# Input projection of a hybrid transformer layer: context after latents, small parameter work after the first norms, modulation pieces two at a time

## The chip, the cores and the metric

The kernel runs on one core of a Trainium2 chip. The metric is the time of one execution on the device in microseconds (us); less is better. The core has five engines that run side by side, each through its own queue in order: PE (TensorE, matrix products), DVE (VectorE), ACT (ScalarE), POOL (GpSimd) and SP (SyncE, which here only issues transfers). They meet through semaphores.

## The reference

One layer over 512 latent tokens (`x`) with a prefix of 256 context tokens (`ctx`), width 1024. The part that the change touches:

```python
m_lat = jax.nn.silu(c) @ w_mod[l] + b_mod[l]          # 6*1024 columns: shift, scale, gate, twice
m_ctx = jax.nn.silu(c_ctx) @ w_mod[l] + b_mod[l]
h_lat = modulate(rmsnorm(x, norm_mix_g[l]), sh1, sc1)     # t * (1 + scale) + shift
h_ctx = modulate(rmsnorm(ctx, norm_mix_g[l]), csh1, csc1)
p_lat = h_lat @ w_in                                   # columns: q 256, kv 128, kr 32, lru x 512, lru gate 512
p_ctx = h_ctx @ w_in
```

From `p_lat` and `p_ctx` come latent attention (queries of the latents only; keys and values of both) and a bidirectional recurrent block (`lru`), then the output projection, a router and 64 experts with 256 hidden columns each, eight of them per token, and a last norm. Nothing of this computation changes.

## The kernel before

Activations are held transposed: 128 channels on the partitions, eight channel tiles k, and 768 token columns, the 512 of the latents (0 to 511) and the 256 of the context behind them. Every product of the input projection is made from two-part numbers: weights and activations are split into a high and a low part (`split`: a cast, then a subtraction), and `mm3` (L357) makes three products, high·high, high·low and low·high, each in two instructions, one of 512 columns for the latents (L362) and one of 256 for the context (L364).

The first stage goes like this. `load_x` (L252) loads two token tiles into one of six "big" buffers. `norm1` (L293) squares each tile on ACT, makes the inverse root with twelve small DVE instructions (`rsqrt`, L150) and scales the tiles on DVE (L299). `trx` (L323) transposes a channel tile of all its token tiles on PE (L326) and copies it out of PSUM, ACT for even k, DVE for odd (L327). `mod1` (L307) makes the shift and scale columns of two channel tiles from two "big" weight tiles `wm1` (64 small products on PE, L311, then a transpose and two DVE instructions up to `mcolA`, L319). `hmake` (L385) applies them: ACT writes the high part `hH` (L388), POOL the full value `hfull` (L390), DVE their difference `hL` (L392). It does both token groups of a channel tile in one call. `kvproj` (L395) and `qproj` (L400) then add one channel tile into the PSUM tiles `pkv`, `pkr` and `pqq`, which fill all three wide PSUM buffers (`pw`, L228); there is one narrow buffer (`pn`, L231). `wtile` (L342) splits weights.

Afterwards the pool `pH`, with the six big buffers and the transposed activations, is closed (L422), and pools that take its memory are opened. In them lie the weights of the recurrent block's gates (`gv`, 16 loads issued by POOL, L474, split by POOL into `gH`, `gL`), the buffers of the modulation pieces and the temporaries. Then come four full projections of the `lru` columns (`proj`, L366, tiles `pp`, the first one `plx[0]` with weights `wl0`, the second with `wl1`), four of the gate columns for the latents alone (`lgp`, L629), convolutions, gates and scans.

Between them stand 16 modulation pieces (`mod_piece`, L444): each adds 1/8 of the products of 2048 further modulation columns, as four groups of 32 PSUM partitions (L454). In the trace a group is two matmul records. A piece loads the piece after next when it is done (L461), from 1 MB of weights in two transfers. Before the change 13 pieces stand one by one in the code and the last three in `mod_piece(16)` (L705).

SP's queue runs in the order in which the code is written (L109), which is the order of the loads: `x`, `wkv`, the first `wm1` pair, `ctx`, `wq`, three `wm1` pairs, `C2` and `C4` (two further parts of `w_in`). The queues of PE, ACT, DVE and POOL are ordered when the kernel is built, by a planner that takes the ready instruction of the highest priority by its own estimates of times; priority is the place in the code, moved by the offsets in `PRI` (L60). At run time nothing is reordered.

Of the kernel before, what the change touches and what calls it, by code (L numbers as in the profile page):

```python
# [8 lines left out]
F32 = mybir.dt.float32  # L9
# [3 lines left out]
AF = mybir.ActivationFunctionType  # L13
OP = mybir.AluOpType
# [86 lines left out]
def tile_kernel(tc, x, c, ctx, c_ctx, w_mod, b_mod, norm_mix_g, w_in, q_norm_g, w_q_up, kv_norm_g, w_kv_up,  # L101
# [17 lines left out]
    def pick(name, default):  # L119
        return {"A": ACT, "D": DVE, "P": POOL}[ENG.get(name, default)]  # L120
# [5 lines left out]
    def after(ins, other, reason):  # L126
        tc.add_manual_dep(ins, other.name, mybir.DependencyInfo(mybir.DependencyClass.Sync, mybir.DependencyReason.DATA),
                          reason=reason)

    def prio(name):  # L130
        def deco(f):
            def g(*args, **kw):
                off = PRI.get(name, 0)
                if not off:
                    return f(*args, **kw)
                with tc.high_priority(offset=off):
                    return f(*args, **kw)
            return g
        return deco
# [88 lines left out]
    def pw(name="pw"):  # L228
        return ps.tile([P, 1024], F32, tag="w", name=name, bufs=3)
# [31 lines left out]
    def load_win(c0, n):  # L261
        w = raw8("win")
        v = w.rearrange("p (k f) -> p k f", k=KT)[:, :, :n]
        SP.dma_start(v, w_in[0].rearrange("(k p) f -> p k f", p=P)[:, :, c0:c0 + n])
        return v

    wkv = load_win(C_KV, 160)
    wm1 = {}

    def load_wm1(c):  # L270
        for x_ in range(2):
            w = big("wm1").rearrange("p (k f) -> p k f", k=KT)
            SP.dma_start(w, wmv[:, :, x_ * D + c * 256:x_ * D + (c + 1) * 256])
            wm1[c, x_] = w

    load_wm1(0)
    load_x(ctx[0], 2)
    wq = load_win(0, 256)
    for c in range(1, 4):
        load_wm1(c)  # L280
    C2 = load_win(C_LX, 256)
    C4 = load_win(C_LG, 256)

# [37 lines left out]

    @prio("trx")
    def trx(k, t0, t1):  # L323
        pt = pw("pt")
        for t in range(t0, t1):
            PE.transpose(pt[:, (t - t0) * P:(t - t0 + 1) * P], xn[t][:, k * P:(k + 1) * P], ident)  # L326
        (DVE.tensor_copy if k % 2 else ACT.copy)(xnT[:, k, t0 * P:t1 * P], pt[:, 0:(t1 - t0) * P])  # L327

    for k in range(KT):
        trx(k, 0, NT)  # L330
    norm1(NT, NTA)
    pc = pn("pc")
    PE.transpose(pc[:, :P], prow, ident)
    DVE.tensor_copy(pcol[:, :ncol], pc[:, :ncol])
# [22 lines left out]
    def mm3(p, wt, k, first, last, lat=True, cx=True):  # L357
        hv, lv = wt
        for i, (w, m) in enumerate(((hv, hH), (hv, hL), (lv, hH))):
            st, sp = first and i == 0, last and i == 2  # L360
            if lat:
                PE.matmul(p[:, 0:S], w[:, k, :], m[:, k, 0:S], start=st, stop=sp)  # L362
            if cx:
                PE.matmul(p[:, S:ST], w[:, k, :], m[:, k, S:ST], start=st, stop=sp)  # L364
# [4 lines left out]
            mm3(p, wt, k, k == 0, k == KT - 1, cx=cx)  # L369
        return p  # L370

    for k in range(KT):
        trx(k, NT, NTA)
    wqt = []
    for m in range(2):
        z = pK.tile([P, 2, KT, P], F32R, tag=f"qw{m}", name="wqs", bufs=1)
# [4 lines left out]
    wl0 = z  # L381
    pkv, pkr, pqq = pw("pkv"), pw("pkr"), pw("pqq")

    @prio("hmake")
    def hmake(k):  # L385
        tt = hf("hfull")[:, 0:ST]
        for s, a, b in ((0, 0, S), (1, S, ST)):
            ACT.activation(hH[:, k, a:b], xnT[:, k, a:b], AF.Identity, scale=mcolA[:, k, s:s + 1],  # L388
                           bias=mcolS[:, k, s:s + 1])
            pick("hm", "P").tensor_scalar(tt[:, a:b], xnT[:, k, a:b], mcolA[:, k, s:s + 1], mcolS[:, k, s:s + 1],  # L390
                               op0=OP.mult, op1=OP.add)
        DVE.tensor_tensor(hL[:, k, :], tt, hH[:, k, :].bitcast(F32), op=OP.subtract)  # L392

    @prio("kvproj")
    def kvproj(k):  # L395
        mm3(pkv, kvt, k, k == 0, k == KT - 1)
        mm3(pkr, krt, k, k == 0, k == KT - 1)

    @prio("qproj")
    def qproj(k):  # L400
        for m in range(2):
            for i, (w, h_) in enumerate(((wqt[m][0], hH), (wqt[m][0], hL), (wqt[m][1], hH))):
                PE.matmul(pqq[:, m * S:(m + 1) * S], w[:, k, :], h_[:, k, 0:S],
                          start=(k == 0 and i == 0), stop=(k == KT - 1 and i == 2))
# [3 lines left out]
    for c in range(4):  # L408
        if c < 3:
            mod1(c + 1)  # L410
            hmake(2 * c + 2)
            hmake(2 * c + 3)
        kvproj(2 * c)
        if c < 3:
            qproj(2 * c)
        kvproj(2 * c + 1)
        if c < 3:
            qproj(2 * c + 1)
    qproj(6)
    qproj(7)  # L420
    load_brow(1)
    st_H.close()  # L422
    st_Z = ExitStack()
# [60 lines left out]

    @prio("small_params")
    def small_params():
        DVE.tensor_scalar(pcol[:, col["qg"]:col["qg"] + 2], pcol[:, col["qg"]:col["qg"] + 2], SCALE, None, op0=OP.mult)
        DVE.tensor_scalar(bh, pcol[:, col["ba"]:col["ba"] + 16], 0.5, None, op0=OP.mult)
        DVE.scalar_tensor_tensor(sm[0], lam, -1.0, lam, op0=OP.mult, op1=OP.max)
        ACT.activation(sm[1], sm[0], AF.Exp, scale=-1.0)  # L490
        DVE.tensor_scalar(sm[0], sm[1], 2.0, None, op0=OP.add)
        DVE.reciprocal(sm[2], sm[0])
        DVE.tensor_tensor(sm[0], sm[1], sm[2], op=OP.mult)
        DVE.tensor_tensor(sm[1], sm[0], sm[0], op=OP.mult)
        DVE.tensor_scalar(sm[2], sm[1], 1.0 / 17.0, None, op0=OP.mult)
        for nn in (15, 13, 11, 9, 7, 5, 3):
            DVE.scalar_tensor_tensor(sm[2], sm[2], 1.0 / nn, sm[1], op0=OP.add, op1=OP.mult)
        DVE.scalar_tensor_tensor(sm[2], sm[2], 1.0, sm[0], op0=OP.add, op1=OP.mult)
        DVE.tensor_scalar(sm[3], lam, -1.0, 0.0, op0=OP.mult, op1=OP.max)
        DVE.scalar_tensor_tensor(sm[3], sm[2], 2.0, sm[3], op0=OP.mult, op1=OP.add)  # L500
        DVE.tensor_scalar(spp, sm[3], 4.0, None, op0=OP.mult)
        DVE.tensor_scalar(spn, sm[3], -4.0, None, op0=OP.mult)
# [88 lines left out]
    plx = {}  # L591
    plx[0] = proj(wl0)
    wl1 = wtile(C2, P, "l1")
    mod_piece()
    pss = pn("pss")
    for t in range(NTA):
        PE.matmul(pss[:, t:t + 1], sqk[:, t * P:(t + 1) * P], ones[:, 0:1], start=True, stop=True)
# [8 lines left out]
    rsqrt(pL, nr, nv, 10, "rq")  # L606
    conv_b(0)
    plx[1] = proj(wl1)
    mod_piece()
    for i in range(LT):  # L610
        split(gH[:, i], gL[:, i], gvs[i][:, 0:4 * P], "gw")
    wg = wtile(C4, 0, "g0")
# [25 lines left out]
        ACT.activation(h_, h_, AF.Tanh)  # L638
        DVE.scalar_tensor_tensor(x_, h_, 1.0, x_, op0=OP.add, op1=OP.mult)

    mod_piece()
    lgp(0, wg)
    split(kvnH, kvnL, kvr, "kvn")
    for m in range(2):
# [2 lines left out]
    zs = gates_pe(0, 1)  # L647
    conv_b(1)
    gates_ew(0, 1, zs)
    mod_piece()  # L650
    plx[2] = proj(wl2)
    wg = wtile(C4, P, "g1")
    C5 = load_win(C_LG + 256, 256)
    mod_piece()
    zs = gates_pe(1, 0)
    gates_ew(1, 0, zs)
    conv_a(2, plx[2])
    mod_piece()
    lgp(1, wg)
    wl3 = wtile(C3, P, "l3")  # L660
    mod_piece()
    zs = gates_pe(1, 1)
    conv_b(2)
    gates_ew(1, 1, zs)
    mod_piece()
    plx[3] = proj(wl3)
    wg = wtile(C5, 0, "g2")
    wkvraw = raw8("wkvraw")[:, 0:1024]
# [2 lines left out]
    scan(0, 0)  # L671
    scan(0, 1)
    scan(1, 0)
    mod_piece()
    zs = gates_pe(2, 0)
    conv_a(3, plx[3])
    gates_ew(2, 0, zs)
    scan(1, 1)
    mod_piece()
    lgp(2, wg)  # L680
    wg = wtile(C5, P, "g3")
    wqraw = raw8("wqraw").rearrange("p (k h d) -> p k h d", k=2, h=H)
# [2 lines left out]
    for half in range(2):  # L685
        o, i = (wqraw[:, :, :, c0:c0 + 32].rearrange("p k h (a x j) -> p k h a x j", a=2, x=2)[:, :, :, :, x]
                for c0, x in ((DQK, half), (NOPE, 1 - half)))
        for k in range(2):
            POOL.tensor_copy(o[:, k], i[:, k])
    mod_piece()  # L690
    zs = gates_pe(2, 1)
    conv_b(3)
    gates_ew(2, 1, zs)
    mod_piece()
    zs = gates_pe(3, 0)
    gates_ew(3, 0, zs)
# [930 lines left out]
```

## Time and profile before

| | us |
|---|---|
| median of 3 runs | 1115.57 (1115.56 to 1118.78) |
| the profiled execution | 1114.81 |
| its span, first to last instruction | 1112.8 |
| PE busy | 996.2 (90%) |
| DVE, ACT, POOL busy | 484.3, 255.7, 223.4 |
| mean granted PE clock | 0.962 of full speed |

Times in rows count from the span's start. A row of a timeline gives start, duration, engine, line, operation, output and inputs, shapes, how many instructions were merged, and in brackets how long the engine had been idle before and what ended that. Matmuls overlap, so the pace of a stream is read from the starts, not from the durations.

### The profile page before, as it was taken

How to read it: one execution, taken by the hardware profiler on the slowest of the kernel's cores; microseconds unless marked ns; L12 is line 12 of the kernel's file. 1: busy time of each engine (PE TensorE's matmuls, PEld its weight loads, DVE VectorE, ACT ScalarE, POOL GpSimd, SP SyncE). 2: the span in 40 equal slices, each digit the busy share in tenths (PEclk: the TensorE clock that was granted, in tenths of full speed). 3: DMA queues.
4: the chain of work that ended last, by engine and by line, in shares of the span. 5: the costliest groups of instructions: out<-in, count | busy, mean ns of one | idle time of the engine just before them, and what ended most of it. 6: DMA issues, size and time to landing. Idle time of an engine off the chain costs nothing. (4 is left out here: it accounts for less than half of the span.)

```text
span 1112.8 us, 17435 instructions
## 1 busy us (share of the span) xinstructions
PE 996.2 (90%) x6813; PEld 515.6 (46%) x6813; DVE 484.3 (44%) x1064; ACT 255.7 (23%) x468; POOL 223.4 (20%) x219
## 2 busy tenths in 40 slices
PE   3899989799989998999999999999999999995482
PEld 2687654567779853443443344333333333331131
DVE  5527594988765865223222232222322223220065
ACT  3433545756661210011000110000100001000011
POOL 3382341346100001111111111111111111110001
PEclk9899999889999999999999999999999999997797
DMA  9834644200009543999999898989879999989694
GB/s 294 266 96 154 206 161 133 77 1 1 1 2 365 226 195 132 416 394 417 419 409 360 333 390 346 395 323 399 339 289 401 399 413 414 399 319 414 251 421 186
DMA packets 75404, 310.34 MB, mean 279 GB/s; under 512 B 12747, under 2 KB 31234, under 8 KB 48442
## 3 DMA queue, kind: packets, MB, share of 16 engines
q1 hardware_dynamic: 60412, 271.79, 63.2%
q0 software_dynamic: 13936, 34.26, 8.1%
q10 hardware_dynamic: 974, 3.17, 0.8%
q8 instruction: 54, 0.88, 0.3%
q14 instruction: 28, 0.23, 0.1%
HBM read 293.31 MB, written 30.29 MB: 291 GB/s over the span
## 5 line engine op out<-in xcount | busy, mean ns | idle before, releaser
L1382 PE MATMUL gu<-wgu,hT 128*32 128x512 f32 (+2 forms) x2160 | 333.0, 597 | 11.1 <-DMA wgu<-in_exp_w_up_dram 10.4
L1382 PEld LDWEIGHTS gu<-wgu,hT 128*32 128x32 f32 (+2 forms) x2160 | 105.4, 120 | 230.2 <-issue 225.9
L1403 PE MATMUL dn<-wd,aT 128*32 128x512 f32 (+2 forms) x1080 | 169.1, 596 | 16.6 <-ACT aT L124 15.4
L1385 DVE TENSOR_TENSOR act<-act,gu 128x256 f32<-128x256 f32 (+1 forms) x46 | 19.4, 421 | 297.8 <-ACT act L1384 297.8
L1384 ACT ACTIVATE act<-gu 128x256 f32<-128x256 f32 (+1 forms) x46 | 17.7, 385 | 511.7 <-PE gu L1382 511.7
L1332 POOL DMA_INDIRECT hg<-h2d,bix x46 | 47.6, 1034 | 425.9 <-issue 310.4
L1406 DVE SCALAR_TENSOR_TENSOR y<-dn,bw,g2b 128x1024 f32<-128x1024 f32 (+1 forms) x46 | 59.0, 1283 | 138.2 <-PE dn L1403 138.2
L1403 PEld LDWEIGHTS dn<-wd,aT 128*32 128x32 f32 (+2 forms) x1080 | 48.7, 119 | 100.8 <-issue 78.8
L1407 POOL DMA_INDIRECT yd<-y,biy x46 | 46.8, 1017 | 191.9 <-DVE y L1406 182.5
L1370 PEld LDWEIGHTS tr<-ident,hg 128*128 128x128 f32 (+1 forms) x368 | 39.9, 141 | 37.1 <-issue 34.1
L1370 PE MATMUL tr<-ident,hg 128*128 128x128 f32 (+1 forms) x368 | 49.7, 278 | 1.3 <-DVE tb L1084 1.3
L1548 PE MATMUL fs<-yl,ident 128*128 128x512 f32 x64 | 32.1, 654 | 20.3 <-DMA yl<-yd 18.1
L829 PE MATMUL pTr<-ident,P 128*128 128x128 f32 x192 | 30.7, 300 | 9.8 <-DVE P L820 7.7
L1306 DVE TENSOR_TENSOR sv<-iot,posR 128x256 bf16<-128x256 f32 (+3 forms) x93 | 37.1, 411 | 0.0
L812 DVE TENSOR_REDUCE nm<-pS 128x1 f32<-128x768 f32 x32 | 30.3, 951 | 11.2 <-PE pS L810 10.8
L124 ACT COPY PT<-pTr 128x384 f32<-128x384 f32 x64 | 28.0, 482 | 29.0 <-PE pTr L829 28.7
L124 ACT COPY hT<-tr 128x512 f32<-128x512 f32 (+1 forms) x46 | 26.9, 584 | 34.0 <-PE tr L1370 32.5
L840 PE MATMUL po<-PT,vsb 128*64 128x128 f32 x384 | 30.8, 299 | 1.7 <-ACT PT L124 1.7
L454 PE MATMUL pmx<-wm,csil 128*32 128x512 f32 x128 | 31.9, 606 | 0.0
L124 DVE COPY hT<-tr 128x512 f32<-128x512 f32 (+1 forms) x46 | 31.3, 680 | 0.0
L1548 PEld LDWEIGHTS fs<-yl,ident 128*128 128x128 f32 x64 | 12.7, 208 | 39.8 <-DMA yl<-yd 20.4
L829 PEld LDWEIGHTS pTr<-ident,P 128*128 128x128 f32 x192 | 24.1, 153 | 14.8 <-issue 7.7
(473 smaller groups left out, 1472.9 us busy)
## 6 DMA issues: line engine op xcount, KB each, us to landing
wgu<-in_exp_w_gate_dram SPq DMA_DIRECT2D x64, 1024.0 KB
wgu<-in_exp_w_up_dram SPq DMA_DIRECT2D x64, 1024.0 KB
wd<-in_exp_w_down_dram SPq DMA_DIRECT2D x64, 1024.0 KB
wm<-in_w_mod_dram SPq DMA_DIRECT2D x32, 512.0 KB
yl<-yd SPq DMA_DIRECT2D x16, 1024.0 KB
wm<-in_w_mod_dram SPq DMA_DIRECT2D x8, 1024.0 KB
win<-in_w_in_dram SPq DMA_DIRECT2D x5, 1024.0 KB
xz<-in_x_dram SPq DMA_DIRECT2D x4, 512.0 KB
```

The costliest lines, as they stand in the source:

```text
L124: (e.copy if e is ACT else e.tensor_copy)(dst, src)
L454: PE.matmul(pm[32 * g:32 * g + 32, :], csil[:, kk, :], wmp[n, g // 2][:, (g % 2) * 512:(g % 2 + 1) * 512], start=(kk == 0), stop=(kk == KT ...
L829: PE.transpose(p[:, j * P:(j + 1) * P], Pm[u][:, k * P:(k + 1) * P], ident)
L840: PE.matmul(po[i][64 * hh:64 * hh + 64, t * P:(t + 1) * P], vsb[:, k, 2 * i + hh, :], PTt[i, t, hh][:, k, :], start=(k == 0), stop=(k == N ...
L1306: DVE.tensor_tensor(sv[:, :, c:c + w], iot[:, u:u + w][:, None, :].to_broadcast([P, NT, w]), col_[:, :, None].to_broadcast([P, NT, w]), op ...
L1332: POOL.indirect_dma_start(out=b.hg[0:m], out_offset=None, in_=h2d, in_offset=bass.IndirectOffsetOnAxis(ap=b.ix[0:m, :1], axis=0), bounds_c ...
L1370: PE.transpose(p[:, i * m:(i + 1) * m], b.hg[0:m, (i0 + i) * P:(i0 + i + 1) * P], ident[0:m, 0:m])
L1382: PE.matmul(p[c:c + w, :], b.hT[:, k, c:c + w], wg[n][:, :, k, :], start=(k == 0), stop=(k == KT - 1))
L1403: PE.matmul(p[c:c + w, n0:n0 + 512], b.aT[:, k, c:c + w], wd_[n][:, k, n0:n0 + 512], start=(k == 0), stop=(k == 1))
L1406: DVE.scalar_tensor_tensor(y[0:m], p[0:m], b.w[0:m], g2b[0:m], op0=OP.mult, op1=OP.mult)
L1407: ins = POOL.indirect_dma_start(out=yd, out_offset=bass.IndirectOffsetOnAxis(ap=b.iy[0:m, :1], axis=0), in_=y[0:m], in_offset=None, bounds ...
L1548: PE.matmul(p[:, n0:n0 + 512], ident, yl[t, k][:, n0:n0 + 512], start=(k == 0), stop=(k == 3))
```

## The change

The load of `wkv` goes behind the first `wm1` pair and the load of `ctx` behind the last. The norm, the transposes, the modulation and the key/value products of the context are taken out of the latents' loop and follow it, channel tile by channel tile; the context's transposes use the narrow PSUM buffer. Four small DVE instructions that begin the parameter work of the recurrent block get a dependency on the second `hL` of the latents. The pieces that stood one by one now stand in six pairs, and the last four are left for `mod_piece(16)`.

```diff
-    wkv = load_win(C_KV, 160)
...
     load_wm1(0)
-    load_x(ctx[0], 2)
+    wkv = load_win(C_KV, 160)
     wq = load_win(0, 256)
     for c in range(1, 4):
         load_wm1(c)
+    load_x(ctx[0], 2)
     C2 = load_win(C_LX, 256)
...
-        pt = pw("pt")
+        pt = (pw if t0 == 0 else pn)("pt")
...
         trx(k, 0, NT)
-    norm1(NT, NTA)
...
-    for k in range(KT):
-        trx(k, NT, NTA)
...
+    hm = []
+
     @prio("hmake")
-    def hmake(k):
+    def hmake(k, s=0):
         tt = hf("hfull")[:, 0:ST]
-        for s, a, b in ((0, 0, S), (1, S, ST)):
...
+        a, b = ((0, S), (S, ST))[s]
...
+        hm.append(DVE.tensor_tensor(hL[:, k, a:b], tt[:, a:b], hH[:, k, a:b].bitcast(F32), op=OP.subtract).ins)
...
-    def kvproj(k):
-        mm3(pkv, kvt, k, k == 0, k == KT - 1)
-        mm3(pkr, krt, k, k == 0, k == KT - 1)
+    def kvproj(k, s=0):
+        mm3(pkv, kvt, k, k == 0, k == KT - 1, lat=(s == 0), cx=(s == 1))
+        mm3(pkr, krt, k, k == 0, k == KT - 1, lat=(s == 0), cx=(s == 1))
...
-        kvproj(2 * c)
-        if c < 3:
-            qproj(2 * c)
-        kvproj(2 * c + 1)
-        if c < 3:
-            qproj(2 * c + 1)
-    qproj(6)
-    qproj(7)
+        for k in (2 * c, 2 * c + 1):
+            kvproj(k)
+            qproj(k)
+
+    norm1(NT, NTA)
+    for k in range(KT):
+        trx(k, NT, NTA)
+    for k in range(KT):
+        hmake(k, 1)
+        kvproj(k, 1)
     load_brow(1)
     st_H.close()
...
+            after(ins.ins, hm[1], "not between the first norms")
...
     plx[0] = proj(wl0)
     wl1 = wtile(C2, P, "l1")
-    mod_piece()
...
     plx[1] = proj(wl1)
-    mod_piece()
+    mod_piece(2)
...
-    mod_piece()
     lgp(0, wg)
...
     gates_ew(0, 1, zs)
-    mod_piece()
+    mod_piece(2)
     plx[2] = proj(wl2)
```

The pieces further down are changed in the same way: a pair stands before `lgp(1)`, before `plx[3]`, before `lgp(2)` and before the gates of tile 3; the single calls between them are gone.

## Rows read from the trace of the kernel before

**Rows 1.** Stages: busy time (instructions) of PE, PEld, DVE, ACT, POOL; clock; DMA share; GB/s

```profile
12.00:40.00 28.00, 16.11 (x137) 11.45 (x141) 23.27 (x70) 12.37 (x23) 8.98 (x10) 0.88 1.02 336
40.00:73.65 33.65, 33.65 (x325) 27.69 (x316) 12.16 (x20) 11.28 (x17) 22.00 (x32) 1.00 0.59 183
73.65:196.00 122.35, 118.66 (x569) 74.74 (x568) 75.71 (x103) 54.57 (x60) 44.18 (x28) 0.97 0.47 150
...
375.00:1112.80 737.80, 666.41 (x4568) 264.47 (x4566) 233.32 (x623) 77.53 (x172) 99.07 (x94) 0.97 0.88 351
```

**Rows 2.** PE's timeline, first 40 us

```profile
21.28 1.57 PE L326 MATMUL pt<-ident,xz 128*128 128x128 f32 x6 [3.78 <-DVE xz L299]
...
25.50 1.94 PE L311 MATMUL pm<-wm,csil 128*32 128x128 f32 x60
...
33.08 2.73 PE L326 MATMUL pt<-ident,xz 128*128 128x128 f32 x10 [4.64 <-DVE xz L299]
...
37.98 0.61 PE L362 MATMUL pkv<-hH,wh 128*128 128x512 f32 x1
```

**Rows 3.** DVE's timeline, first 110 us

```profile
10.05 0.17 DVE L296 TENSOR_SCALAR ssq<-ssq 128x2 f32<-128x2 f32 x1 [3.86 <-ACT junk L295]
...
12.23 0.16 DVE L162 SCALAR_TENSOR_TENSOR rstd<-rs0b,rstd 128x2 f32<-128x2 f32 x1
...
15.13 2.31 DVE L489 SCALAR_TENSOR_TENSOR sm<-pcol 128x8 f32<-128x8 f32 x1
...
20.48 1.41 DVE L299 TENSOR_SCALAR xz<-xz,rstd 128x1024 f32<-128x1024 f32 x2
...
28.33 0.15 DVE L319 SCALAR_TENSOR_TENSOR mcolA<-pmT,pcol 128x4 f32<-128x4 f32 x1
...
83.35 3.23 DVE L527 SCALAR_TENSOR_TENSOR u<-pp,pcol,u 128x510 f32<-128x510 f32 x6 [11.45 <-ACT u L522]
...
108.55 0.95 DVE L242 TENSOR_TENSOR ul<-u,uh 128x768 fp32r<-128x768 f32 x1
```

**Rows 4.** Stages again, one stretch of 3 us, columns as in rows 1

```profile
33.00:36.00 3.00, 2.88 (x14) 1.80 (x14) 3.00 (x4) 1.76 (x5) 1.33 (x2) 0.50 1.02 336
```

**Rows 5.** ACT's timeline, start

```profile
12.07 1.06 ACT L295 ACTIVATE junk<-xz 128x1024 f32<-128x1024 f32 x1
```

**Rows 6.** POOL's timeline, first 110 us

```profile
13.88 1.10 POOL L124 CAST wh<-win 128x1024 fp32r<-128x1024 f32 x1 [8.95 <-DMA win<-in_w_in_dram]
...
18.79 1.54 POOL L242 TENSOR_TENSOR krl<-win,krh 128x128 fp32r<-128x128 f32 x3 [1.01 <-DVE krh L124]
...
34.67 2.06 POOL L390 TENSOR_SCALAR hfull<-xnT,mcolA,mcolS 128x256 f32<-128x256 f32 x2 [4.31 <-ACT xnT L327]
...
61.82 0.99 POOL L471 MEMSET gv<- 128x512 f32 x2 [1.10 <-issue]
...
74.81 2.42 POOL L242 TENSOR_TENSOR wl<-win,wh 128x1024 fp32r<-128x1024 f32 x1
...
84.36 2.34 POOL L242 TENSOR_TENSOR wl<-win,wh 128x1024 fp32r<-128x1024 f32 x1
106.51 6.96 POOL L242 TENSOR_TENSOR qnL<-qr,qnH 128x512 fp32r<-128x512 f32 x2 [19.81 <-DVE qnH L124]
```

**Rows 7.** PE's timeline, 70 to 87 us

```profile
73.65 0.39 PE L362 MATMUL pp<-hH,qnH 128*128 128x512 f32 x1
...
83.21 1.50 PE L597 MATMUL pss<-ones,wall 128*128 128x1 f32 x12
...
86.64 0.77 PE L362 MATMUL pp<-hH,wh 128*128 128x512 f32 x1
```

**Rows 8.** PE's timeline, a lone group and the product behind it; two whole pieces in a row

```profile
107.13 1.04 PE L454 MATMUL pmx<-wm,csil 128*32 128x512 f32 x2
108.10 0.51 PE L362 MATMUL pp<-hH,wl 128*128 128x512 f32 x1
...
150.34 1.92 PE L454 MATMUL pmx<-wm,csil 128*32 128x512 f32 x16
```

More of the change, by code (lines that the diff above doesn't have):

```diff
@@ L382, in tile_kernel @@
     pkv, pkr, pqq = pw("pkv"), pw("pkr"), pw("pqq")
+    hm = []
     @prio("hmake")
-    def hmake(k):
+    def hmake(k, s=0):
         tt = hf("hfull")[:, 0:ST]
-        for s, a, b in ((0, 0, S), (1, S, ST)):
[L388 to L392, printed above, removed]
+        a, b = ((0, S), (S, ST))[s]
+        ACT.activation(hH[:, k, a:b], xnT[:, k, a:b], AF.Identity, scale=mcolA[:, k, s:s + 1],
+                       bias=mcolS[:, k, s:s + 1])
+        pick("hm", "P").tensor_scalar(tt[:, a:b], xnT[:, k, a:b], mcolA[:, k, s:s + 1], mcolS[:, k, s:s + 1],
+                           op0=OP.mult, op1=OP.add)
+        hm.append(DVE.tensor_tensor(hL[:, k, a:b], tt[:, a:b], hH[:, k, a:b].bitcast(F32), op=OP.subtract).ins)
     @prio("kvproj")
-    def kvproj(k):
-        mm3(pkv, kvt, k, k == 0, k == KT - 1)
-        mm3(pkr, krt, k, k == 0, k == KT - 1)
+    def kvproj(k, s=0):
+        mm3(pkv, kvt, k, k == 0, k == KT - 1, lat=(s == 0), cx=(s == 1))
+        mm3(pkr, krt, k, k == 0, k == KT - 1, lat=(s == 0), cx=(s == 1))
     @prio("qproj")
@@ L486, in small_params @@
     def small_params():
-        DVE.tensor_scalar(pcol[:, col["qg"]:col["qg"] + 2], pcol[:, col["qg"]:col["qg"] + 2], SCALE, None, op0=OP.mult)
-        DVE.tensor_scalar(bh, pcol[:, col["ba"]:col["ba"] + 16], 0.5, None, op0=OP.mult)
-        DVE.scalar_tensor_tensor(sm[0], lam, -1.0, lam, op0=OP.mult, op1=OP.max)
+        for ins in (
+                DVE.tensor_scalar(pcol[:, col["qg"]:col["qg"] + 2], pcol[:, col["qg"]:col["qg"] + 2], SCALE, None, op0=OP.mult),
+                DVE.tensor_scalar(bh, pcol[:, col["ba"]:col["ba"] + 16], 0.5, None, op0=OP.mult),
+                DVE.tensor_scalar(sm[3], lam, -1.0, 0.0, op0=OP.mult, op1=OP.max),
+                DVE.scalar_tensor_tensor(sm[0], lam, -1.0, lam, op0=OP.mult, op1=OP.max)):
+            after(ins.ins, hm[1], "not between the first norms")
         ACT.activation(sm[1], sm[0], AF.Exp, scale=-1.0)
@@ L498, in small_params @@
         DVE.scalar_tensor_tensor(sm[2], sm[2], 1.0, sm[0], op0=OP.add, op1=OP.mult)
-        DVE.tensor_scalar(sm[3], lam, -1.0, 0.0, op0=OP.mult, op1=OP.max)
         DVE.scalar_tensor_tensor(sm[3], sm[2], 2.0, sm[3], op0=OP.mult, op1=OP.add)
@@ L653, in tile_kernel @@
     C5 = load_win(C_LG + 256, 256)
-    mod_piece()
     zs = gates_pe(1, 0)
@@ L657, in tile_kernel @@
     conv_a(2, plx[2])
-    mod_piece()
+    mod_piece(2)
     lgp(1, wg)
     wl3 = wtile(C3, P, "l3")
-    mod_piece()
     zs = gates_pe(1, 1)
@@ L664, in tile_kernel @@
     gates_ew(1, 1, zs)
-    mod_piece()
+    mod_piece(2)
     plx[3] = proj(wl3)
@@ L673, in tile_kernel @@
     scan(1, 0)
-    mod_piece()
     zs = gates_pe(2, 0)
@@ L678, in tile_kernel @@
     scan(1, 1)
-    mod_piece()
+    mod_piece(2)
     lgp(2, wg)
@@ L689, in tile_kernel @@
             POOL.tensor_copy(o[:, k], i[:, k])
-    mod_piece()
     zs = gates_pe(2, 1)
@@ L693, in tile_kernel @@
     gates_ew(2, 1, zs)
-    mod_piece()
+    mod_piece(2)
     zs = gates_pe(3, 0)
     gates_ew(3, 0, zs)
-    mod_piece()
     wk4 = wkvraw.rearrange("p (h c f) -> p c h f", h=H, c=2)
```

## The prediction

> **What bounds the kernel now.** I read the stages first. From 40 us to the start of attention PE is the bound: it is busy for all of 33.65 us and then for 118.66 of 122.35 us, while DVE, ACT and POOL are busy for 36, 34 and 65% and for 62, 45 and 36%. From 12 to 40 us it is not: PE works 16.11 of 28 us, and the transfers run all the time, at 336 GB/s [rows 1]. The expert stage (375 us to the end) follows with PE and transfers both near full. Its loads are issued as its own buffers come free, so it should start earlier by whatever is gained before it. The question is thus how early PE's stream of products can begin, and what would hole it.
>
> PE's own timeline shows what the beginning waits for. The first product of the projection starts at 37.98 us. Before it lie a wait of 3.78 us for the scaled latents (to 21.28), `mod1(0)` at 25.50, and a wait of 4.64 us for the scaled context (to 33.08) [rows 2]: `hmake` makes both token groups of a channel tile at once, so the first latent product waits for the context. The wait before 21.28 is seen in DVE's timeline. The inverse root of the first two tiles takes 2.34 us (10.05 to 12.39). The next two are scaled only from 20.48 on, because small parameter instructions stand between the steps of their inverse root, one of them with 2.31 us for 128x8 elements [rows 3]. And gaps cost twice: in 33 to 36 us the granted clock is 0.50, the lower of the two levels, after 3 us in which PE did nothing [rows 2, 4].
>
> **The start, step by step.** From here on the times are estimates from those rows. The last latent tile has landed at 12.07 [rows 5]; with 336 GB/s a 1,024 KB transfer takes 3.1 us. In the new order the first `wm1` pair lands at 18.3, `wkv` (640 KB) at 20.3, `wq` at 23.4, the next pairs at 29.6, 35.8 and 42.0, `ctx` at 45.1, `C2` and `C4` at 48.2 and 51.3.
>
> Without the parameter instructions, and with `wkv` not yet there, the first two tiles are scaled by 14.0 (12.39 plus some 1.4 us, as the pair at 20.48 took [rows 3]), the second inverse root takes 2.4 us like the first, and scaling starts near 16.5, transposes at 17.3. `mod1(0)` takes 1.94 us [rows 2] from 18.3, and from its end (27.44) to `mcolA` (28.33 plus 0.15) it is 1.1 us [rows 3], so the modulation columns are there at 21.4. Next is `wkv`, which now comes late: POOL's splits run from 13.88 to 20.33, of which 1.0 us is a wait [rows 6], so 5.4 to 6.4 us, and from 20.3 they end at 26. A first product can run near 23, but an unbroken stream begins at 26 to 27, where it began at 37.98: 11.5 us earlier.
>
> **Does the stream hold?** The stretch from 37.98 to 73.65, where the first full projection starts [rows 7], is 35.7 us of PE work without a hole [rows 1]. All of it stays; the 16 transposes of the context come in from before 37.98: in rows 2 ten take 2.73 us at the lower clock, so I take 2.7 us for all at the higher. The number of products and weight loads is the same, as each 512- and 256-column instruction loaded its own weights before. 26.5 + 35.7 + 2.7 = 64.9, less 1.0 us for the first products that run between 23 and 26.5, plus 0.5 us where the second `wm1` pair (29.6, plus 2 us of products, 1.1 us, and `hmake`) comes later than two channel tiles are worked off. The third and fourth pairs land before PE gets to them. That gives 64.4 for the start of the first full projection, **9.3 us earlier**. Bounds: 12.0 (all of the gain at the start kept) and 4 (waits as long as the one of 4.64 us in rows 2 come back).
>
> The context is worked under this cover: two squares on ACT, twelve small DVE instructions and two scalings bring it to about 50.2. The narrow PSUM buffer is single, so a channel tile needs its two transposes, its copy and the two hand-overs one after the other, some 1.1 us; eight end at 59. POOL's 256-column `hmake` takes 1.03 us [rows 6], so the last ends at 60 and the last `hL` at 60.4. The context's 48 products of 256 columns take 5.7 us by the pace of the first full projection: 24 times 768 columns from 73.65 to 83.21, less one piece of modulation (0.96 us, below), 8.6 us [rows 7]. They are PE's last, so they need not start before 58.7, and PE, with 64.4, still ends after POOL. Without that cover the context's chain would show in full, 15 us from landing to end. The wide PSUM buffers are all held until `pkv`, `pkr` or `pqq` is copied out; `pqq` is now done first, and ACT, busy 11.28 of 33.65 us [rows 1], can copy it beneath the context's products. The subtraction for `hL`, now 16 instead of eight instructions, lies on DVE, busy 36% there.
>
> **The queues that things move past.** On SP the two `ctx` loads pass `wq` and six `wm1` loads and need a buffer that `mod1(1)` frees near 32; behind them wait `C2` and `C4`, whose weights are needed at 64. POOL's queue is what is late next. It begins the recurrent block's weights when the pool is closed, at 61.82, issues 16 loads, and only then, at 74.81 for 2.42 us, makes the low part of `wl1` [rows 6] for the projection at 86.64: 9.4 us of slack [rows 7]. The close barely moves (60.5 for 61.8), since it now waits for the context. So that low part is ready at 75.9, and PE wants it at 64.4 + 8.6 (first projection) + 3.4 (the sums from 83.21 to 86.64 [rows 7]) = 76.4. The slack is gone; I count +0.4 us, between 0 and 4. [...] By rows, a 128x1024 subtraction on POOL took 2.34 us at 84.36 beside the convolution (DVE from 83.35 to 86.58), and two of half the size took 3.48 us each from 106.51 on, beside DVE instructions as the subtraction at 108.55 [rows 3, 6]. [...]
>
> **The pieces.** Two whole pieces in a row cost 1.92 us, 0.96 each, so a pair as such brings nothing. A group issued alone, with another product behind it, costs 0.97 us (107.13 to 108.10), as much as four together [rows 8]: each further lone group costs 0.73 us. The trace has 14 lone groups, all among the products of a gate projection `lgp` or of the values. Piece 2 moves from ahead of `lgp(0)` to behind it: four more lone groups, +2.9 us. Piece 12 moves into the last four, of which the trace takes two groups at a time: -1.0. Together **+1.9**; bounds -10 (all pairs whole) and +17 (three pairs that were whole fall apart, 24 groups).
>
> **Sum.** -9.3 + 0.4 + 1.9 = -7.0 us against the profiled execution of 1114.81, which is its span of 1112.8 and 2.0 around it: 1107.8. The median of the runs is 0.8 above the profiled one, hence **1108.5**. About 0.3%, 3.3 us, is what a measurement of this kernel can tell from no change.
>
> **The rivals.** (a) *The order written into PE's queue makes it wait for the context.* The queues are fixed at build time from estimates. If the context's transposes stand ahead of the last latent products, PE sits from 43 or 44 to 50; the waits of 4.64 and 3.78 us in rows 2 are of this kind, and the half clock follows. 6 us go: 1114.5, no change. Against it: the context's work has a later place in the code. (b) *POOL is slowed,* as above: the two-input subtractions at 106.51 ran at three times the time per column of the one at 84.36 [rows 6], so the low part of `wl1` takes 7.2 instead of 2.4 us, is ready at 80.7 and PE waits 4.3 us: -9.3 + 4.3 + 1.9 gives 1112.5, no change. The convolution row is against it. (c) *Lone groups decide, and it gets slower.* The sum is -7.0, so from ten more lone groups on the gain is gone. If 16 of the 24 groups in the first, third and fifth pair fall apart, because a gate projection is ready beside them on PE, it is +11.7 - 7.0: 1120. For it: PE's front is earlier against the transfers, so the orders shift, and pairs give longer runs to break. Against it: two pieces in a row came whole twice. (d) *The pairs come whole*, also behind `lgp`: -9.3 + 0.4 - 10 gives 1096; half of it 1101.
>
> **Chances.** Forecast 0.54 (1104 to 1112), (d) 0.11, together faster 0.65; (a) 0.12 and (b) 0.06, together no change 0.18; (c) 0.17, slower. The range reaches from half of (d), 1099, to nearly all of (c), 1119, which leaves out less than 2 in 10.
>
> **What to look for.** First unbroken products at 26 to 27, `plx[0]` at 64; transposes of the context after 50, without an idle PE ahead of them; the low part of `wl1` near 76 with at most a short wait; lone groups about 16; later stages alike, 7 us earlier. I am wrong if PE stands still between 40 and 64, if the pieces take over 36 or under 26 us, or if the end does not move with the start of attention.

## The result: 1.1% slower, and the profile after

The changed kernel takes 1128.99 us (median, 1125.36 to 1131.14), the kernel before 1115.57 beside it: ratio 1.011, interval 1.0094 to 1.0127, 12 to 13 us slower where 7 us less were forecast. The profiled execution took 1131.14 us, with a span of 1129.2 (before 1114.81 and 1112.8), PE busy 1005.2 us for 996.2 and DVE 496.4 for 484.3.

The stages come first, cut at the same events as before. Columns as in [rows 1].

```profile
12.00:40.00 28.00, 22.33 (x197) 15.68 (x198) 17.69 (x55) 8.96 (x15) 9.33 (x10) 0.94 1.10 351
40.00:70.83 30.83, 29.24 (x256) 22.69 (x254) 14.81 (x41) 14.34 (x25) 11.56 (x16) 1.00 0.32 105
70.83:211.00 140.17, 126.59 (x567) 77.30 (x568) 88.08 (x105) 54.62 (x61) 51.78 (x44) 0.93 0.45 147
391.40:1129.20 737.80, 666.81 (x4569) 264.48 (x4567) 233.38 (x623) 77.61 (x172) 98.89 (x94) 0.97 0.88 351
```

Against [rows 1] the stretch up to the first full projection is 2.8 us shorter (70.83 for 73.65). The stretch from there to attention is 17.8 us longer (140.17 for 122.35), and in it PE stands still for 13.6 us where it was 3.7, at a granted clock of 0.93 instead of 0.97. The expert stage takes the same 737.80 us: it only starts later. So nearly the whole loss lies between 71 and 211 us; from there to the expert stage another 1.4 us are added (180.40 for 179.00). PE's timeline names the first part of it:

```profile
25.28 0.47 PE L361 MATMUL pkv<-hH,wh 128*128 128x512 f32 x1 [1.10 <-POOL krl L242]
...
70.83 0.50 PE L361 MATMUL pp<-hH,qnH 128*128 128x512 f32 x1 [1.25 <-ACT wall L586]
...
82.50 0.77 PE L361 MATMUL pp<-hH,wh 128*128 128x512 f32 x1
...
84.75 0.80 PE L361 MATMUL pp<-hH,wl 128*128 128x512 f32 x1 [0.62 <-POOL wl L242]
...
98.48 0.76 PE L543 MATMUL pg<-uh,gH 128*128 128x512 f32 x1 [6.54 <-DVE rqb L160]
```

The first product comes 12.7 us earlier than in [rows 2], the first projection 2.8, the second (82.50 for 86.64 in [rows 7]) 4.1. Then PE waits 6.54 us before the first gates. The row names a step of an inverse root as what it waited for; DVE's timeline shows what stood there:

```profile
82.95 1.79 DVE L152 TENSOR_SCALAR rqi<-nv 128x10 int32<-128x10 int32 x1
84.77 0.52 DVE L154 TENSOR_SCALAR rqj<-rqi 128x10 int32<-128x10 int32 x1
85.33 8.86 DVE L159 TENSOR_TENSOR rqa<-rqj 128x10 f32<-128x10 f32 x1
...
94.51 3.23 DVE L530 SCALAR_TENSOR_TENSOR u<-pp,pcol,u 128x510 f32<-128x510 f32 x6
...
97.77 0.56 DVE L124 CAST uh<-u 128x768 fp32r<-128x768 f32 x1
```

An instruction on 128x10 elements takes 8.86 us, and its twin at 97.65 takes 0.16. The convolution (L530), which before ran ahead of this chain, at 83.35 [rows 3], now stands behind it, and `uh`, which the gates need, comes at 98.3. POOL's timeline beside it:

```profile
82.31 2.39 POOL L242 TENSOR_TENSOR wl<-win,wh 128x1024 fp32r<-128x1024 f32 x1
84.60 1.20 POOL L124 CAST gH<-gv 128x512 fp32r<-128x512 f32 x2
85.73 2.53 POOL L242 TENSOR_TENSOR gL<-gv,gH 128x512 fp32r<-128x512 f32 x2
88.19 1.17 POOL L124 CAST gH<-gv 128x512 fp32r<-128x512 f32 x2
89.32 2.54 POOL L242 TENSOR_TENSOR gL<-gv,gH 128x512 fp32r<-128x512 f32 x2
91.82 2.33 POOL L242 TENSOR_TENSOR wl<-win,wh 128x1024 fp32r<-128x1024 f32 x1
```

POOL splits weights without a gap from 82.31 to 94.15. DVE's first held step ends at 84.74, where POOL's first subtraction ends (84.70); the long one ends at 94.19, where the stream ends. Before, the stream lay 7.5 us earlier (the low part of `wl1` at 74.81 [rows 6], here at 82.31) and the chain came after it.

The second part is among the pieces. There are 18 lone groups, 14 before; the extra ones are the first four of eight that start from 113.84 to 124.12, from piece 2, beside `lgp(0)`. Behind a later wait for `uh`, of the fourth convolution, two lone groups run at half clock (0.50 from 175 to 181 us). PE's timeline, with the same wait of the kernel before below it:

```profile
113.84 1.04 PE L455 MATMUL pmx<-wm,csil 128*32 128x512 f32 x2
...
175.48 0.80 PE L543 MATMUL pg<-uh,gH 128*128 128x512 f32 x1 [3.24 <-DVE uh L124]
...
177.48 1.92 PE L455 MATMUL pmx<-wm,csil 128*32 128x512 f32 x2
...
180.05 1.71 PE L455 MATMUL pmx<-wm,csil 128*32 128x512 f32 x2
```

```profile
164.08 0.51 PE L540 MATMUL pg<-uh,gH 128*128 128x512 f32 x1 [0.51 <-DVE uh L124]
```

Until the end of piece 1 the kernel has lost 7.9 us (107.44 for 99.55, the product that follows), by the end of the last piece 15.2 (210.47 for 195.22), and at the start of the expert stage 16.4.

### The profile page after: what moved, and what is told of

Same layout as the page of the kernel before. It is cut to its first block, busy times and chain, and to the rows that moved or that the text cites. A ratio compares the mean times of both kernels' runs of the same rounds, so it can differ in the third digit from the quotient of the medians.

```text
span 1129.2 us, 17460 instructions
## 1 busy us (share of the span) xinstructions
PE 1005.2 (89%) x6813; PEld 516.5 (46%) x6813; DVE 496.4 (44%) x1072; ACT 256.2 (23%) x468; POOL 220.4 (20%) x219
## 5 line engine op out<-in xcount | busy, mean ns | idle before, releaser
L1399 PE MATMUL dn<-wd,aT 128*32 128x512 f32 (+2 forms) x1080 | 169.1, 596 | 16.5 <-ACT aT L124 15.2
L1544 PE MATMUL fs<-yl,ident 128*128 128x512 f32 x64 | 32.4, 656 | 19.9 <-DMA yl<-yd 17.8
L455 PE MATMUL pmx<-wm,csil 128*32 128x512 f32 x128 | 36.0, 615 | 0.0
```

What stands on the lines that cost most here:

```text
L1399: PE.matmul(p[c:c + w, n0:n0 + 512], b.aT[:, k, c:c + w], wd_[n][:, k, n0:n0 + 512], start=(k == 0), stop=(k == 1))
L1544: PE.matmul(p[:, n0:n0 + 512], ident, yl[t, k][:, n0:n0 + 512], start=(k == 0), stop=(k == 3))
```

## The experiments

Theories: (1) DVE's step is held by POOL's unbroken stream, and the convolution is queued behind it; (2) the context's chain comes late, because its squares wait for a buffer; (3) the pairs cost by themselves. In the table the kernel before is the one run beside each kernel (median 1115.57 beside the changed kernel, 1117.0 to 1117.2 beside the others).

| run | us | ratio to before (95%) |
|---|---|---|
| changed kernel | 1128.99 | 1.0110 (1.0094 to 1.0127) |
| e1_junk | 1126.58 | 1.0089 (1.0070 to 1.0108) |
| e2_singles | 1119.55 | 1.0020 (1.0010 to 1.0029) |
| e3_pairs_only | 1124.80 | 1.0069 (1.0051 to 1.0088) |
| e4_gw_off_pool | 1120.97 | 1.0040 (1.0025 to 1.0056) |
| e5_first_piece | 1125.52 | 1.0077 (1.0062 to 1.0091) |
| e6_conv_first | 1120.90 | 1.0039 (1.0024 to 1.0054) |
| e7_small_later | 1114.85 | 0.9983 (0.9972 to 0.9994) |
| e9_half_stream | 1127.39 | 1.0100 (1.0080 to 1.0120) |
| c2_junk_singles_gw | 1112.66 | 0.9965 (0.9955 to 0.9976) |
| c3_early_ctx | 1112.56 | 0.9960 (0.9947 to 0.9972) |
| c4_pairs_back | 1121.09 | 1.0035 (1.0016 to 1.0054) |
| c5_order_not_gw | 1112.11 | 0.9963 (0.9952 to 0.9973) |
| c6_late_pairs | 1116.07 | 0.9991 (0.9977 to 1.0004) |
| c7_early_pairs | 1116.57 | 1.0006 (0.9991 to 1.0020) |

A caution on single profiles: c2 and c6 are the same program up to the scans, and their first full projections start at 66.60 and 68.57. Starts are compared to within 2 us only; the verdicts rest on the medians. The changed kernel's own median comes from four runs, with an interval of 1.8 us to either side, so a difference of 2 us to it (e1, e9) is not clear of noise.

### The held step: e4, e6, e9

e4 moves the gate weights' splits off POOL:

```diff
-    ... "gw.h": "P",
-    "gw.l": "P", ...
+    ... "gw.h": "A",
+    "gw.l": "D", ...
```

> The changed kernel with the four gate weights' splits on ScalarE (high part) and VectorE (low part) in place of GpSimd, nothing else. Theory (VectorE's 128x10 step of 8.86 us is held by GpSimd's unbroken stream): that step takes under 0.5 us once GpSimd is idle, the convolution follows some 6 us earlier, TensorE's wait of 6.54 us shrinks to under 2, and the time is 1119 to 1124 us, less what the added VectorE work costs. Rival (the long step waits for something else, a product or a transfer): it stays near 9 us and the time at 1129 or above.

1120.97, as theory 1 said. The step takes 0.17 us, PE waits 0.62 us at the gates instead of 6.54. Another DVE instruction is caught now, beside what is left of POOL's stream (DVE, then POOL):

```profile
81.71 5.43 DVE L242 TENSOR_TENSOR gL<-gv,gH 128x512 fp32r<-128x512 f32 x1 [1.49 <-ACT gH L124]
```

```profile
81.84 4.74 POOL L242 TENSOR_TENSOR wl<-win,wh 128x1024 fp32r<-128x1024 f32 x2
```

A subtraction that takes 0.65 us in the same kernel (two in 1.29 us) took 5.43 and ended 0.56 us after POOL's two: it did its own work only then.

e6 leaves the stream and changes DVE's order alone:

```diff
+    cv = conv_a(0, plx[0])
...
+        after(ins.ins, cv.ins, "convolution first")
```

> The changed kernel with one added order: the first convolution's last VectorE step comes ahead of the two steps that open the reciprocal root chain. Theory (the loss there is a queue order on VectorE behind GpSimd's stream): the convolution ends near 87 instead of 97.7, some small step or cast behind it is held until GpSimd's stream ends near 94, TensorE's wait before the first gates falls from 6.54 to about 4: 1125 to 1127 us. Rival (VectorE's order does not matter since GpSimd holds it either way): 1129.

1120.90: more than expected, and as much as e4. DVE's timeline, then POOL's:

```profile
79.78 3.23 DVE L530 SCALAR_TENSOR_TENSOR u<-pp,pcol,u 128x510 f32<-128x510 f32 x6 [8.62 <-ACT u L525]
...
83.27 1.18 DVE L124 CAST uh<-u 128x768 fp32r<-128x768 f32 x1
...
84.86 0.94 DVE L242 TENSOR_TENSOR ul<-u,uh 128x768 fp32r<-128x768 f32 x1
85.73 3.04 DVE L154 TENSOR_SCALAR rqj<-rqi 128x10 int32<-128x10 int32 x1
...
89.35 5.38 DVE L160 SCALAR_TENSOR_TENSOR rqb<-rqa,nv 128x10 f32<-128x10 f32 x1
```

```profile
83.92 2.35 POOL L124 CAST gH<-gv 128x512 fp32r<-128x512 f32 x2
86.24 2.50 POOL L242 TENSOR_TENSOR gL<-gv,gH 128x512 fp32r<-128x512 f32 x2
...
92.33 2.38 POOL L242 TENSOR_TENSOR wl<-win,wh 128x1024 fp32r<-128x1024 f32 x1
```

The same chain is still held for 8.4 us (3.04 and 5.38, the last ending at 94.73, the stream at 94.71), but the convolution, the cast and the subtraction are through, and PE does not wait at the gates at all. Here `uh` and `ul` got in at a boundary of POOL's instructions, and POOL waited instead: its pair of casts took 2.35 us for 1.20. So the stall cost only through what was queued behind it: some 8 us of the loss.

e9 moves two of the four splits (a name without an entry in `ENG` goes to ACT and DVE):

```diff
-        split(gH[:, i], gL[:, i], gvs[i][:, 0:4 * P], "gw")
+        split(gH[:, i], gL[:, i], gvs[i][:, 0:4 * P], "gw" if i < 2 else "gx")
```

> The changed kernel with two of the four gate weights' splits off GpSimd instead of all four. Theory (VectorE's step is held until GpSimd's unbroken stream ends, so a shorter stream holds it shorter): the stream ends 3.6 us earlier, near 90.5, and the VectorE step that is caught ends within 0.5 us of that; TensorE's wait before the first gates is 2.5 to 3.5 us instead of 6.54; 1124 to 1126 us, half way to the kernel with all four moved. Rival (moving any split helps by taking load from GpSimd alone, the caught step keeps its 8.9 us): 1128 to 1129.

The mechanism is as expected, the gain smaller: 1127.39 lies between the two forecasts, and the time alone, not clear of the changed kernel's, would not decide. DVE's timeline:

```profile
82.40 3.57 DVE L242 TENSOR_TENSOR gL<-gv,gH 128x512 fp32r<-128x512 f32 x1 [9.44 <-ACT gH L124]
...
86.27 5.02 DVE L152 TENSOR_SCALAR rqi<-nv 128x10 int32<-128x10 int32 x1
```

POOL's stream ends at 91.26 (its last subtraction runs for 2.38 us from 88.88), the caught step at 91.29, and the wait before the gates is 3.77 us for 6.54. The stream ended 0.8 us later than expected: one pair of its casts took 1.64 us for 1.20, beside the DVE subtraction that the edit added.

### The pairs: e2, e3, e5, c4, c6, c7

e2 puts the 13 single calls back into the changed kernel, e3 puts the pairs alone into the kernel before:

```diff
-    mod_piece(2)
+    mod_piece()
```

> The changed kernel with the modulation pieces one by one again at their places of before; load order, norm order and small parameter work stay as changed. Theory (the pairs cost twice: the piece that stood between the first projection and the norm sums kept VectorE's convolution ahead of the reciprocal root chain, and a pair with nothing between leaves lone products): the convolution runs first, TensorE's wait of 6.54 us at 98.5 goes, 14 lone products instead of 18: 1112 to 1117 us. Rival (GpSimd's stream stalls VectorE in either order, and the pairs are free): 1126 to 1129.

> The kernel before with the pairs alone; load order, norm order and small parameter work as before. Theory (the pairs are the loss): 4 to 10 us slower than before, 1119 to 1126, with the reciprocal root chain ahead of the convolution on VectorE and its two-operand step long beside GpSimd. Rival (the loss comes from the later context, pairs are free): 1115 to 1117.

e2 gives back 9.4 of the 12 to 13 us, short of what was expected, and e3 loses 7.7 against 1117.1, without any wait at the first gates: there the chain does stand ahead of the convolution, but POOL's stream had ended (86.24) before it began (86.37), and the step takes 0.17 us. So the pairs cost by themselves. In e2 the planner does put the convolution first, as it did before the change, but PE still waits 4.15 us at the gates: the next step is caught, ahead of the cast of `uh` (the stream ended at 93.87):

```profile
83.67 3.24 DVE L530 SCALAR_TENSOR_TENSOR u<-pp,pcol,u 128x510 f32<-128x510 f32 x6
86.82 7.08 DVE L152 TENSOR_SCALAR rqi<-nv 128x10 int32<-128x10 int32 x1
93.81 0.55 DVE L124 CAST uh<-u 128x768 fp32r<-128x768 f32 x1
```

e5 puts back one piece alone, between the first projection and the norm sums:

```diff
     wl1 = wtile(C2, P, "l1")
+    mod_piece()
     pss = pn("pss")
...
-    mod_piece(2)
+    mod_piece()
```

> The changed kernel with one modulation piece back between the first full projection and the norm sums, and one after the second projection; all other pieces stay in pairs. Theory (the first pair costs by VectorE's order, the later ones by lone products and by less cover for the waits before the gates): the convolution stands ahead of the reciprocal root chain, TensorE's wait before the first gates is 4 us instead of 6.54, the lone products stay near 18: 1122 to 1126 us. Rival (only the first place matters): 1119 to 1120, as with all pieces single.

1125.52, as expected: the order flips (wait 4.26 us) and the rest of the pairs' price stays. c4 has the pairs without the long hold of the chain (the edits of e1 and e4; 0.98 us of wait at the first gates); c2 below is the same with single pieces:

> The context squares in their own buffer and the gate weight splits off GpSimd, but the pieces in pairs as changed. Theory (apart from VectorE's order, the pairs cost 4 to 7 us: four more lone products and less cover for the waits before the gates): 1117 to 1120 us against 1112.7 with single pieces. Rival (without GpSimd's stream the pairs are free): 1112 to 1114.

1121.09 against 1112.66: 8.4 us, more than the 4 to 7 expected. Four lone groups at 0.73 us [rows 8] are 2.9 of them. c6 and c7 pair one half of the pieces each, on top of c2:

```diff
-    mod_piece()
     zs = gates_pe(2, 0)
...
-    mod_piece()
+    mod_piece(2)
     lgp(2, wg)
...
-    mod_piece()
     zs = gates_pe(2, 1)
...
-    mod_piece()
+    mod_piece(2)
     zs = gates_pe(3, 0)
...
-    mod_piece()
```

This is c6; c7 has the changed kernel's calls ahead of these places and single ones here.

> The three edits together, with the pieces of the second half alone (from the scans on) in pairs. Theory (the late pairs take the single piece away that covers TensorE's wait for the cast of the convolution, which grows from 0.54 to 2 to 3 us, and half clock follows it): 4 to 5 us slower than with single pieces, 1116 to 1118 us, lone products as before. Rival (the pairs cost by lone products alone, which are the early pairs'): 1112 to 1114.

> The three edits together, with the pieces of the first half alone in pairs. Theory (the early pairs put two pieces beside the first latent gate projection, which has products for neither: four more lone products, 2.9 us, and 1 to 2 us of VectorE's order): 1115.5 to 1117.5 us. Rival (the early pairs are the whole loss): 1120 to 1121.

Late pairs cost 3.4 us (4 to 5 expected), early ones 3.9, together 7.3 of the 8.4. The late price shows in the wait for the cast of the fourth convolution: 0.51 us before, 0.54 in c2, 0.67 in c7, but 3.34 in c6 and 3.24 in c4. Of c6, then c7:

```profile
156.64 1.04 PE L457 MATMUL pmx<-wm,csil 128*32 128x512 f32 x2
...
161.45 0.80 PE L545 MATMUL pg<-uh,gH 128*128 128x512 f32 x1 [3.34 <-DVE uh L124]
```

```profile
159.91 1.92 PE L457 MATMUL pmx<-wm,csil 128*32 128x512 f32 x2
...
162.49 1.45 PE L457 MATMUL pmx<-wm,csil 128*32 128x512 f32 x2
...
165.03 0.50 PE L545 MATMUL pg<-uh,gH 128*128 128x512 f32 x1 [0.67 <-DVE uh L124]
```

Wherever PE waits for the cast, the gates behind it start 6.4 to 6.6 us after the gates before it (157.66 to 164.08 before, 154.92 to 161.45 in c6), whatever PE does meanwhile. With single pieces two lone groups lie in that time, with late pairs one; the other is then done later, at its full price. In c2 and c7 the half clock falls into this covered time as well (1.92 and 1.45 us for a group in c7), in c4 and c6 behind the wait, where it costs. Stages of 4 us, in c2 with its wait at 158.93 and in c4 with its wait at 165.23, columns as in [rows 1]:

```profile
154.60:158.60 4.00, 3.79 (x6) 0.66 (x4) 4.00 (x8) 0.77 (x1) 2.02 (x3) 0.66 0.39 108
```

```profile
164.60:168.60 4.00, 3.37 (x7) 1.56 (x7) 4.00 (x6) 0.00 (x0) 4.00 (x1) 0.50 0.00 0
```

The number of lone groups under the wait goes with the pieces in every kernel here; the place of the half clock does not. In e1, which has the pairs, it falls under the cover and the wait is short; in e2, which has single pieces, there is none (a clock of 1.00 from 160.94 to 167.36) and the wait is long. PE's timeline of e1, then of e2:

```profile
170.85 1.92 PE L457 MATMUL pmx<-wm,csil 128*32 128x512 f32 x2
...
174.20 0.50 PE L545 MATMUL pg<-uh,gH 128*128 128x512 f32 x1 [0.71 <-DVE uh L124]
```

```profile
167.36 0.50 PE L543 MATMUL pg<-uh,gH 128*128 128x512 f32 x1 [2.09 <-DVE uh L124]
```

The second group is thus worth about 1.15 us of cover (a wait of 3.24 us in the changed kernel, where the clock over that time is 0.93, and of 2.09 in e2). How much of the 3.4 us belongs to the half clock, and whether the pairs decide where it falls, is not shown.

### The start: e1, e7, c3

e1 lets the squares write their unused output elsewhere than into `hf`, whose two buffers `hmake` uses for all channel tiles:

```diff
+        jb = big("junk") if t0 == NT else None
         for t in range(t0, t1):
-            ACT.activation(hf("junk"), xn[t], AF.Square, accum_out=ssq[:, t:t + 1])
+            j_ = jb[:, (t - t0) * D:(t - t0 + 1) * D] if t0 == NT else hf("junk")
+            ACT.activation(j_, xn[t], AF.Square, accum_out=ssq[:, t:t + 1])
```

> The changed kernel, with one edit: the squares of the context's norm write their unused output into a buffer of their own and no longer into the two that the hidden state's halves rotate through. Theory (the context chain is held by that rotation): the squares start at about 45 us instead of 52.74, the first full projection at 63 to 65 instead of 70.83, the wide pool closes near 61 instead of 68.7, and since VectorE's stall behind GpSimd moves with them as a whole, the time is 1121 to 1124 us. Rival (the context is not what the first full projection waits for): the projection stays at 70.8 and the time at 1129.

1126.58, 2.4 us less where 5 to 8 were expected, and not clear of noise. c4 adds the same edit to e4 and its time is the same (1121.09 for 1120.97), though in both pairs of profiles the first projection comes 2.1 to 2.5 us earlier (68.69 for 70.83, 67.96 for 70.49). So the scratch buffer is worth between nothing and 2.4 us. In the changed kernel the first square waits for a `hL` of the latents, in e1 it does not; but then DVE's queue takes over (ACT of the changed kernel, then DVE of e1):

```profile
52.74 1.06 ACT L295 ACTIVATE junk<-xz 128x1024 f32<-128x1024 f32 x1 [0.17 <-DVE hL L391]
```

```profile
50.79 0.15 DVE L321 SCALAR_TENSOR_TENSOR mcolA<-pmT,pcol 128x4 f32<-128x4 f32 x1
50.85 0.16 DVE L298 TENSOR_SCALAR ssq<-ssq 128x2 f32<-128x2 f32 x1
```

The squares are done at 48 (ACT from 45.80), and their sums wait until 50.85, behind the last modulation columns. c3 adds to the three edits of c2 the context's norm, transposes and hidden state at an earlier place in the code:

```diff
+        if c == 2:
+            norm1(NT, NTA)
...
+            if c == 3:
+                for j in range(4 * (k - 6), 4 * (k - 6) + 4):
+                    trx(j, NT, NTA)
+                    hmake(j, 1)
```

> The three edits together (context squares in their own buffer, single pieces, gate weight splits off GpSimd), and the context's norm, transposes and hidden state written among the latents' last products instead of behind them. Theory (the context is a serial tail of 8 us through transposes, ScalarE, GpSimd and VectorE, beside which TensorE still has products of the latents to do): the first full projection starts 2 to 4 us earlier than with the three edits alone (66.60), 1109 to 1111 us. Rival (the modulation weights' arrival near 50 and the products left after it set the projection's start): no change, 1112 to 1113.

The theory fell, the rival stands: 1112.56. In c3 the sums again follow the last columns on DVE (51.06), and between the last columns and the first projection PE waits for only 0.41 us. PE's timeline around the transposition of the last columns, of the changed kernel and of the kernel before:

```profile
50.42 0.27 PE L316 MATMUL pmT<-ident,mrow 128*128 128x128 f32 x1
```

```profile
55.76 0.27 PE L316 MATMUL pmT<-ident,mrow 128*128 128x128 f32 x1
```

From there to the first projection it takes 17.9 us before (to 73.65), 20.4 in the changed kernel (to 70.83) and 18.3 in c2 and c3 (48.31 to 66.60, 50.60 to 68.91). The last columns come only 5.3 us earlier (7.4 in c2's profile), though the first product comes 12.7 us earlier. What would bring them earlier was not tried.

e7 is the small parameter work alone, in the kernel before (the four dependencies on the second `hL`, as in the change):

> The kernel before with the small parameter work alone moved behind the second hidden state part. Theory (it lies beside other work before and after): 1115 to 1118 us, no difference that can be told. Rival (it held the first norm chain on VectorE): the scaling of the latents and with it the first transposes come 3 to 5 us earlier and the time falls by up to 3 us, 1112 to 1114.

1114.85, 0.17% less, at the edge of what can be told; the first product stays at 37.80 and the first projection at 74.04, since PE waits for the context there. But its trace shows what held the latents' second inverse root. Its chain takes 6.3 us before (14.12 to 20.43), 5.8 in e7 (13.26 to 19.05) and 2.1 in the changed kernel (13.54 to 15.67). Without the parameter work a step of the chain itself is held in e7, up to the end of a subtraction on POOL (14.20 to 16.55); in the changed kernel POOL has nothing to split yet (its first cast starts at 20.30). DVE's timeline of e7:

```profile
14.38 2.18 DVE L159 TENSOR_TENSOR rs2a<-rs2j 128x2 f32<-128x2 f32 x1
```

So moving the parameter work alone frees little of this chain; in the changed kernel the late load of `wkv` freed it. The profile does not show where the 0.17% (1.9 us) would be.

### All three: c2 and c5

c2 has the edits of e1, e2 and e4; c5 those of e1, e2 and e6.

> The changed kernel with three edits together: the context's squares into a buffer of their own, the pieces one by one, the gate weights' splits off GpSimd. Theory (three causes that add up, of which the single pieces and the splits share TensorE's wait of 4 us before the gates): 1119.6 less 2.4 less 3 to 4: 1113 to 1115 us, at or below the kernel before. Rival (the splits on VectorE and ScalarE push back the gates there as much as they free): 1118 to 1120.

> The context squares in their own buffer, single pieces, and the first convolution ahead of the norm sums' steps on VectorE by an added order; the gate weight splits stay on GpSimd. Theory (what counts is that the convolution and the cast of its result get through VectorE before GpSimd's stream catches a step): no wait before the first gates, 1112 to 1114 us, as with the splits moved. Rival (the cast or its low part are caught instead, or the norm's row products come late): 1115 to 1118.

Both beat the kernel before: 1112.66 and 1112.11, ratios 0.9965 and 0.9963. In c5 POOL keeps its splits, DVE's chain is still held for 5.39 us, and the gates start at 85.95 without a wait.

## Why the prediction was wrong

**The start** was nearly right: a first product near 23 and the stream from 26 to 27 were forecast; the first product came at 25.28, and the next ones ran from 27.19. (The pause that ended at 33.08 us was 4.64 us long [rows 2]. The clock was 1.00 up to 31 us, 0.72 from 31 to 32 and 0.50 from 32 on: it fell during the pause, by an estimate from these shares some 3 us after its start.) The reason was right in part: the second inverse root did shrink, but by the late `wkv`; moving the parameter work alone did little (e7).

**"Does the stream hold?"** It did not, and this is the first step that failed. The prediction put 64.4 for the first projection; it was 70.83. Columns as in [rows 1]:

```profile
24.00:28.00 4.00, 1.68 (x7) 1.03 (x6) 2.98 (x5) 3.77 (x5) 3.70 (x6) 0.98 1.10 348
28.00:32.00 4.00, 4.00 (x14) 2.45 (x14) 3.59 (x11) 0.21 (x1) 0.00 (x0) 0.60 1.10 350
...
36.00:40.00 4.00, 3.12 (x17) 1.81 (x14) 1.81 (x5) 1.52 (x2) 2.02 (x2) 1.00 1.10 358
```

PE idles 2.3 us in the first stretch, has a clock of 0.60 in the second and idles 0.9 us in the third, where `mod1(1)` must pass through DVE and ACT before the next channel tiles can start. Taking the 35.7 us of [rows 7] as a block that only has to be started carried over a stream that was unbroken because it began late: by 37.98 the columns of the first tiles had been ready for 9.5 us (28.48 [rows 3]). Started earlier, the stream meets the columns one pair at a time, and the last pair moved by 5.3 us, not by 12. The second error in this step is the context "under this cover": scaled by 50.2 in the prediction, by 59.94 in the run, since a scratch buffer tied the squares to the latents' last two `hL`. e1, which unties them, gains at most 2.4 us, because the sums then wait in DVE's queue for the last modulation columns.

**POOL's queue** is the step that cost most. The pool was closed at 68.8 instead of 60.5, and the low part of `wl1` ready at 84.70 instead of 75.9. PE's wait for it was only 0.62 us (predicted 0.4). But the prediction asked whether POOL would be slowed, left a hold of VectorE out of the sum, and took the convolution beside POOL's subtraction at 84.36 as evidence. The convolution reads PSUM and one SBUF operand; in every run here it takes 3.23 or 3.24 us, beside POOL's stream (at 83.35 before) and at rest (at 94.51 in the changed kernel) alike. So it told nothing of instructions whose operands all lie in SBUF. The row that told of the hold was in [rows 3], the 2.31 us for 128x8 elements at 15.13, and the prediction read it as a slow parameter instruction: it ended at 17.44, where POOL's subtraction beside it ended, at 17.41. POOL's timeline before:

```profile
15.06 2.35 POOL L242 TENSOR_TENSOR wl<-win,wh 128x1024 fp32r<-128x1024 f32 x1
```

In the changed kernel the hold of 8.86 us outlasted seven instructions of GpSimd in a row (85.73 to 94.15). By e4 and e6 the step costs 8 us.

**The pieces** were right in the count of lone groups (18, with 16 forecast, four of them as named) and wrong in the sum: +1.9 against 7.7 (e3) and 8.4 (c4 against c2). The term left out is the cover: single pieces left one more lone group under a wait for DVE, and the late pairs moved it out (c6, 3.4 us, of which about 1.15 are this group; the half clock lies in the rest, but the pairs are not shown to decide its place). Piece 12 gave nothing back. And the piece between the first projection and the norm sums had set DVE's order: without it the chain went ahead of the convolution, and e5, which puts it back alone, turns the order round. Of the early pairs' 3.9 us, 2.9 are the four lone groups, at the 0.73 us of [rows 8].

**The rivals.** (a) did not occur: between 40 and 64 us PE never waited over 0.2 us. (b) had the right pair of engines with the roles exchanged. (c) had the right sign, but its ten more lone groups were four; the order in DVE's queue, which decided, was in none of them.

**The sum.** Against 1117 the new order with the three repairs is worth 4 to 5 us (c2, c5; 9.3 forecast). The held step costs 8 us by e4 and e6, and 5.5 where the scratch buffer is repaired (c4 against e1); the pairs cost 8, the scratch buffer between nothing and 2.4. By addition that is 9 to 14 us slower, against 12 to 13 measured. The parts overlap, as e2 shows.

## What to carry to other kernels

Before work on GpSimd is moved, look at what VectorE does beside it: a chain of tiny SBUF instructions can stand still until GpSimd's run ends (8.86 us for one of 128x10 elements in the changed kernel), so put whatever others wait for ahead of such a chain (e6), or take work out of the run (e4). Work that looks misplaced between two stages may be the cover of a wait or the reason for an order; before it is moved, list the waits behind it. And an earlier start is worth only as much as the last input that the stream needs moves with it.

## What the runs showed of the hardware

While GpSimd worked through weight splits without a gap, VectorE instructions whose operands all lie in SBUF were held, several of them until GpSimd's run ended: 8.86 us for 128x10 with two inputs in the changed kernel, 7.08 us in e2 and 5.02 us in e9 for 128x10 with one input (int32), 0.16 to 0.17 us each when GpSimd was idle (at 97.65 in the changed kernel, at 87.44 before). In four kernels the release falls within 0.04 us of the end of GpSimd's stream (94.19 and 94.15, 93.90 and 93.87, 94.73 and 94.71, 91.29 and 91.26). At some boundaries inside the run VectorE got in (in e6 at 88.77, behind a pair of subtractions that ended at 88.74), and at some of these GpSimd waited (a pair of casts in 2.35 us for 1.20); which boundary does it was not settled. The convolution, which reads PSUM and one SBUF operand, was not held (3.23 us).
